# Seven of the gate layers' 32 row pairs computed in seven products, and the last down sets' combined products added to the residual earlier

## The chip, the cores and the metric

The kernel runs on one core of a Trainium2 chip. The metric is device time in microseconds (us) of one execution; the time before is 2294.47, the median of 3 runs (2294.33 to 2295.38). The profile is of one further execution.

## What is computed

The reference is a two-layer decoder trunk for 256 positions of width 2048, all in float32. What matters here is the second half of each layer:

```python
hn = rmsnorm(h, ln_mlp_g[i])
h = h + jnp.square(jax.nn.relu(hn @ mlp_w_up[i])) @ mlp_w_down[i]     # 2048 -> 8192 -> 2048
gate = jax.nn.sigmoid(rmsnorm(h, ln_ple_g[i]) @ ple_w_gate[i])        # 2048 -> 2048
h = h + gate * (p[i] @ ple_w_proj[i])                                 # 256 -> 2048
```

The first half of layer 0 is a recurrent and pooling mixer, that of layer 1 an attention mixer; a final rmsnorm closes the kernel.

## The kernel before

**Sets, pairs and steps.** A product with a 2048-row weight matrix is cut into *sets*: `mm_set` computes all 256 positions for 1024 output columns over eight *row pairs* (p = 0 to 7) of 256 weight rows. A layer's up product has eight sets, the down product eight (quarter q of the hidden width, column half n2), the gate two (`ple`, n2 = 0 and 1). A pair's weights arrive in one 1 MB load (tile `raw`, three buffers, SyncE's queue). Each pair is computed in *steps*; step s works on one weight *half* of two 512-column slices.

**The split.** A float32 product is made of three fp32r products, so every half is split: ScalarE copies it rounded into `hi` (`emit_hi`, L204), VectorE subtracts that from it into `lo` (`emit_lo`, L211). TensorE takes three products per output tile: x_hi·hi, x_lo·hi, x_hi·lo (L710, L711, L712). `hi` and `lo` have four buffers each, so the hi of step s can be written only when the products of step s-4 have read theirs.

**Plain and seven-product pairs.** A *plain* pair has two steps of 12 products, 24 in all. A pair listed in `own` is done in a Strassen-like way with seven combined products instead of eight: 21 products in four steps (3, 6, 6, 6). The third and fourth step use sums of weight blocks that VectorE makes first (`first`, L735; `second`, L740 and L741), and sums of x blocks (`ph["S"]`). Its halves are 1, 2, 2, 2 slices wide, so seven slices are split, not four. The four combined products of the last own pair are put together in `out1` to `out3` (L757 to L770) into two tiles w.

**The order of the work.** The kernel is scheduled by hand: `run` goes through the steps, and each engine does its instructions strictly in the order in which they are written:

```python
splits("sum", s + SUMS)      # weight sums, four steps ahead
splits("hi", ahead)          # hi of step s + 2
splits("lo", s)
fn(halves[s]["hi"], halves[s]["lo"])      # the products of step s
... later.pop(now) ...       # what after(n, f) has put off to this step
splits("lo", ahead)          # lo of step s + 2
```

`order` gives the pairs of a set: `TWO` is 0, 1, 4, 5, 2, 6, 3, 7 with own pairs 2 and 3, `THREE` is 0, 4, 1, 5, 2, 6, 3, 7 with own pairs 1, 2 and 3. The gate sets are plain, in order 0 to 7, with the small projection (`proj`, two steps) ahead of the fifth pair and the row scale (`rstd_of`) ahead of the sixth.

**Ends of sets.** `h_out` adds a down set's results to the residual h: `wide` (L831) adds w one and two steps after the set, `adds` (L838) the plain banks three and four steps after. Where the next product needs it (q = 3), `x_after` then transposes h (L808 on TensorE), scales it into the next x (`high` L411, `low` L874) and sums squares. For sets with own pairs in the next product, `keep` and `sums` make the S operands; before, only the sets of `out_sets` did that here. A gate set ends in `tanh` and `add` (L1056 to L1061; in layer 1 `last`, L1026 to L1034).

Of the kernel before, what the change touches and what calls it, by code (L numbers as in the profile page):

```python
# [112 lines left out]
def trunk(ctx: ExitStack, tc: tile.TileContext, a: dict, out: bass.AP):  # L113
# [573 lines left out]
    def wtiles():  # L687
        return utile().rearrange("p a b -> p (a b)").rearrange("p (n c) -> p n c", c=512), ph["w2"]

    def mm_set(src, order, X, post, own=(), S=None, between={}, hooks={}, by_n=None):  # L690


        B, n_set = ph["B"], ph["sets"]
        ph["sets"] += 1
        order = list(order)
        roles = {r: (i + 4 * n_set) % 8 for i, r in enumerate(PLAIN[0] + PLAIN[1] + OWNR)}
        begun = set()
        owned = [p for p in order if p in own]
        last = {r: owned[-1] if r in OWNR else order[-1] for r in roles if owned or r not in OWNR}
        w = {}  # L700

        def acc_of(r):
            while len(B) <= roles[r]:
                B.append(bank())
            return B[roles[r]]

        def product(r, x, hi, lo, n, end):
            b = acc_of(r)
            x_hi, x_lo = x
            pe.matmul(b, lhsT=x_hi, rhs=hi[:, n, :], start=r not in begun, stop=False, skip_group_check=True)  # L710
            pe.matmul(b, lhsT=x_lo, rhs=hi[:, n, :], start=False, stop=False, skip_group_check=True)  # L711
            pe.matmul(b, lhsT=x_hi, rhs=lo[:, n, :], start=False, stop=end, skip_group_check=True)  # L712
            begun.add(r)

        def A(p, k, t):
            x = X(2 * p + k)
            return x[:, t * P:(t + 1) * P], x[:, T + t * P:T + (t + 1) * P]

        def plain(p, k):
            def fn(hi, lo):  # L720
                for n in range(2):
                    for t in range(2):
                        product(PLAIN[t][n], A(p, k, t), hi, lo, n, k == 1 and p == order[-1])
                if k == 1 and p == order[-1]:
                    post(w.get("w"), [[acc_of(PLAIN[t][n]) for n in range(2)] for t in range(2)])
            return fn

        def own_fns(p):
            def sx(x):
                v = ph["S"][S][p][:, x - 1, :]  # L730
                return v[:, :P], v[:, P:]

            def first(raw):
                t = w["t"] = slot()
                dve.tensor_tensor(t, raw[:, 0::3, :], raw[:, 1:2, :].to_broadcast([P, 2, 512]), op=OP.add)  # L735
                return t

            def second(raw):
                t = slot()
                dve.tensor_tensor(t[:, 0], w["t"][:, 0], raw[:, 3], op=OP.add)  # L740
                dve.tensor_tensor(t[:, 1], t[:, 0], raw[:, 2], op=OP.add)  # L741
                return t

            def fn(*what):
                def f(hi, lo):
                    for n, (r, x) in enumerate(what):
                        product(r, x() if callable(x) else sx(x), hi, lo, n, False if r in PLAIN[0] + PLAIN[1] else p == last[r])
                    if p == owned[-1] and what[0][0] == "P6":
                        for d, g in enumerate((out1, out2, out3)):
                            after(d, g)  # L750
                return f
            return [(0, 1, None, fn(("Q1", lambda: A(p, 0, 0)))),
                    (2, 2, None, fn(("Q2", lambda: A(p, 1, 0)), ("P3", 4))),
                    (0, 2, first, fn(("Q5", 1), ("P7", 3))),
                    (0, 2, second, fn(("P6", 2), ("P4", lambda: A(p, 1, 1))))]

        def out1():  # L757
            w1, w2 = w["w"] = wtiles()
            for to, r in ((w1[:, 0], "Q1"), (w2[:, 0], "P7"), (w2[:, 1], "Q5")):
                act.activation(to, acc_of(r), AF.Copy)  # L760
            dve.tensor_tensor(w1[:, 1], acc_of("P6"), w1[:, 0], op=OP.subtract)

        def out2():
            w1, w2 = w["w"]
            dve.scalar_tensor_tensor(w2[:, 0], w2[:, 0], -1.0, w1[:, 1], op0=OP.mult, op1=OP.subtract)
            dve.tensor_tensor(w1[:, 1], w1[:, 1], w2[:, 1], op=OP.subtract)

        def out3():
            w1, w2 = w["w"]
            dve.scalar_tensor_tensor(w2[:, 1], w2[:, 0], -1.0, w2[:, 1], op0=OP.mult, op1=OP.subtract)  # L770

        def column(p, n):

            def fn(hi, lo):
                for k in range(2):
                    for t in range(2):
                        product(PLAIN[t][n], A(p, k, t), hi, lo, k, k == 1 and p == order[-1])
                if p == order[-1]:
                    splits("lo", state["step"] + 2)
                    by_n(n, [acc_of(PLAIN[t][n]) for t in range(2)])  # L780
            return fn

        for i, p in enumerate(order):
            if by_n and i == len(order) - 2:
                us = [len(loads), len(loads) + 1]
                for q in order[i:]:
                    loads.append({"src": src(q), "nk": 4, "w": 512})
                for n in range(2):
                    for u, q in zip(us, order[i:]):
                        halves.append({"at": (u, slice(n, 4, 2), 2)})  # L790
                        steps.append(("w", len(halves) - 1, column(q, n)))
                return
            if i in between:
                between[i]()
            if i in hooks:
                add_hook(hooks[i])
            parts = own_fns(p) if p in own else [(0, 2, None, plain(p, 0)), (2, 2, None, plain(p, 1))]
            add_blocks(src(p), parts)
# [19 lines left out]

    TWO, THREE = ((2, 3), (0, 1, 4, 5, 2, 6, 3, 7)), ((1, 2, 3), (0, 4, 1, 5, 2, 6, 3, 7))

    def h_out(n2, r, X, gi, sx=None, w_first=True):

        def post(w, banks):
            hb = lambda t, n: h[:, t, n2 * 1024 + n * 512:n2 * 1024 + (n + 1) * 512]

            def wide(t):
                ht = h[:, t, n2 * 1024:(n2 + 1) * 1024].rearrange("p (n c) -> p n c", c=512)
                if r is None:
                    dve.tensor_tensor(ht, ht, w[t], op=OP.add)
                else:  # L830
                    dve.scalar_tensor_tensor(ht, w[t], r[:, t:t + 1], ht, op0=OP.mult, op1=OP.add)  # L831

            def adds(n):
                for t in range(2):
# [4 lines left out]
            if w is not None and X is None:  # L839
# [2 lines left out]
                after(4, lambda: wide(0))  # L842
                after(8, lambda: wide(1))
                return
            at = 0 if w is None else 3
            for t in range(0 if w is None else 2):
                after(1 + t, lambda t=t: wide(t))
            for n in range(2):
                after(at + n, lambda n=n: adds(n))
# [71 lines left out]
    def mlp(l, X, Xn):  # L921
# [66 lines left out]
        for q in range(4):  # L988
            for n2 in range(2):
                post = up_out(q, n2)  # L990
                if q == 0 and n2 == 0:
                    post = (lambda post: lambda w, banks: (after(0, r2_of), post(w, banks)))(post)
                own, order = THREE if q and n2 == 0 else TWO
                mm_set(lambda p, q=q, n2=n2: a["mlp_w_up"][l][q][n2][p], order, X, post, own, 0)
            for n2 in range(2):
                own, order = THREE if n2 and q < 3 else TWO
                mm_set(lambda p, q=q, n2=n2: a["mlp_w_down"][l][n2][8 * q + p], order, H,
                       h_out(n2, R2, Xn if q == 3 else None, G_PLE + 16 * l), own, 1)

    def ple(l, X, Xn):  # L1000
        st = {}
# [12 lines left out]
        def gate(n2):  # L1014
# [2 lines left out]
            gb = lambda n: st["g"][:, n2 * 1024 + n * 512:n2 * 1024 + (n + 1) * 512]  # L1017
            hg = lambda t, n: st["hg"][:, t, n2 * 1024 + n * 512:n2 * 1024 + (n + 1) * 512]

            def last(n, banks):  # L1020

                W = st.setdefault("W", None) or wtiles()
                st["W"] = W if n == 0 else None
                end = n2 == 1 and n == 1
                for t in range(2):
                    act.activation(W[t][:, n], banks[t], AF.Tanh, scale=HALF[:, t:t + 1])  # L1026

                def add(t):
                    dve.scalar_tensor_tensor(W[t][:, n], W[t][:, n], 1.0, eb(t, n), op0=OP.add, op1=OP.mult)
# [1 line left out]
                    last_square(t, n2, n)  # L1031

                def times_gain(t):
                    dve.tensor_tensor(hg(t, n), hb(t, n), gb(n), op=OP.mult)  # L1034
                if end:
                    add(0)
# [9 lines left out]

            def post(w, banks):
                if l == 1:
                    for n in range(2):
                        after(2 * n, lambda n=n: last(n, [banks[t][n] for t in range(2)]))  # L1050
                    return
                W = wtiles()

                def tanh(n):
                    for t in range(2):
                        act.activation(W[t][:, n], banks[t][n], AF.Tanh, scale=HALF[:, t:t + 1])  # L1056

                def add(n):
                    for t in range(2):
# [10 lines left out]
        def load_e():  # L1070
            st["e"] = big(F32, (P, 2, D))
            if l == 1:
                st["g"] = big(F32, (P, 2, D))[:, 0]
                st["hg"] = big(F32, (P, 2, D))
                g = a["gfin"]
                nc.scalar.dma_start(st["g"], g.to_broadcast([P, D]))

# [22 lines left out]
        add_hook(load_e)  # L1100
        for n2 in range(2):
            post, last = gate(n2)
            mm_set(lambda p, n2=n2: a["ple_w_gate"][l][n2][p], range(8), X, post, between={4: lambda n2=n2: proj(n2)},
                   hooks={5: rstd_of} if n2 == 0 else {}, by_n=last if l == 1 and n2 == 1 else None)
        add_hook(ph["close"])

# [341 lines left out]
```

## Time and profile before

| | |
|---|---|
| median of 3 runs | 2294.47 us |
| the profiled execution | 2295.85 us |
| its span, first to last instruction | 2293.8 us |
| TensorE (PE) busy | 2269.0 us, 99% |
| VectorE (DVE) busy | 1797.9 us, 78% |
| ScalarE (ACT) busy | 1340.6 us, 58% |
| DMA, mean | 190 GB/s |
| granted TensorE clock, mean | 0.998 |

PE is TensorE's matmul, PEld its weight load, DVE VectorE, ACT ScalarE, SP SyncE. L204 is line 204 of the kernel. A row of a timeline gives the start (us from the span's start), the length, engine, line, operation, tiles written and read, shape and count; in brackets the idle time ahead of it and what ended it. Matmuls are pipelined: their lengths overlap, and the distance of two starts is what one takes.

### The profile page before, as it was taken

How to read it: one execution, taken by the hardware profiler on the slowest of the kernel's cores; microseconds unless marked ns; L12 is line 12 of the kernel's file. 1: busy time of each engine (PE TensorE's matmuls, PEld its weight loads, DVE VectorE, ACT ScalarE, POOL GpSimd, SP SyncE). 2: the span in 40 equal slices, each digit the busy share in tenths (PEclk: the TensorE clock that was granted, in tenths of full speed). 3: DMA queues.
4: the chain of work that ended last, by engine and by line, in shares of the span. 5: the costliest groups of instructions: out<-in, count | busy, mean ns of one | idle time of the engine just before them, and what ended most of it. 6: DMA issues, size and time to landing. Idle time of an engine off the chain costs nothing.

```text
span 2293.8 us, 30360 instructions
## 1 busy us (share of the span) xinstructions
PE 2269.0 (99%) x11506; PEld 1927.0 (84%) x11506; DVE 1797.9 (78%) x2475; ACT 1340.6 (58%) x1940; POOL 14.6 (1%) x42
## 2 busy tenths in 40 slices
PE   8999999999999999999999999999999999999997
PEld 8998888888888888889889988888888888888886
DVE  6786688988988987856875676688988988988865
ACT  6665565565566565665564454566566565565654
POOL 2000000000000000000000000000000000000000
PEclk9999999999999999999999999999999999999999
DMA  7645555555555555555775224555555555555553
GB/s 259 213 155 179 204 184 202 202 184 200 204 184 196 206 185 199 187 183 204 255 275 177 87 93 159 176 184 200 190 198 196 192 199 194 194 199 191 204 194 129
DMA packets 69539, 436.58 MB, mean 190 GB/s; under 512 B 9872, under 2 KB 14352, under 8 KB 18448
## 3 DMA queue, kind: packets, MB, share of 16 engines
q1 hardware_dynamic: 64832, 427.90, 54.0%
q10 hardware_dynamic: 4560, 6.74, 0.9%
q8 instruction: 90, 1.47, 0.3%
q14 instruction: 57, 0.47, 0.1%
HBM read 432.51 MB, written 2.10 MB: 189 GB/s over the span
## 4 chain that ended last, share of the span: by engine, by line
PE 97%; DVE 1%; DMA 0%; ACT 0%; issue 0%; SPq 0%; DVEq 0%; ACTq 0%
PE ps L712 25%; PE ps L710 25%; PE ps L711 25%; PE ps L295 11%; PE ps L299 3%; PE ps L808 2%; PE ps L1390 1%; PE ps L300 1%; PE ps L1180 1%; PE ps L963 0%; DVE lo L211 0%; DMA raw<-in_ab_w_in 0%; PE ps L1332 0%; PE ps L1330 0%; PE ps L1333 0%; PE ps L588 0%
## 5 line engine op out<-in xcount | busy, mean ns | idle before, releaser
L211 DVE TENSOR_TENSOR lo<-raw,hi 128x1024 fp32r<-128x1024 f32 (+1 forms) x817 | 935.9, 1158 | 159.1 <-ACT hi L204 158.4
L204 ACT ACTIVATE hi<-raw 128x1024 fp32r<-128x1024 f32 (+1 forms) x817 | 813.3, 1008 | 382.8 <-PE ps L711 300.5
L710 PE MATMUL ps<-hi,big 128*128 128x512 f32 x2436 | 954.5, 392 | 0.0
L712 PE MATMUL ps<-lo,big 128*128 128x512 f32 x2436 | 948.8, 389 | 0.0
L711 PE MATMUL ps<-hi,big 128*128 128x512 f32 x2436 | 948.1, 389 | 0.0
L712 PEld LDWEIGHTS ps<-lo,big 128*128 128x128 f32 x2436 | 457.2, 188 | 96.2 <-DVE lo L211 0.6
L711 PEld LDWEIGHTS ps<-hi,big 128*128 128x128 f32 x2436 | 457.5, 188 | 92.9
L710 PEld LDWEIGHTS ps<-hi,big 128*128 128x128 f32 x2436 | 457.4, 188 | 92.8
L204 ACT ACTIVATE hi<-big 128x1024 fp32r<-128x1024 f32 x152 | 161.4, 1062 | 253.3 <-PE ps L711 213.2
L295 PE MATMUL ps<-big,hi 128*128 128x256 f32 x1408 | 264.5, 289 | 7.7 <-ACT hi L204 7.7
L211 DVE TENSOR_TENSOR lo<-big,hi 128x1024 fp32r<-128x1024 f32 x152 | 185.8, 1222 | 90.8 <-ACT hi L204 90.8
L295 PEld LDWEIGHTS ps<-big,hi 128*128 128x128 f32 x1408 | 223.1, 193 | 9.7 <-ACT hi L204 7.7
L295 PE MATMUL ps<-big,lo 128*128 128x256 f32 x704 | 200.5, 285 | 1.0 <-DVE lo L211 0.9
L295 PEld LDWEIGHTS ps<-big,lo 128*128 128x128 f32 x704 | 135.8, 193 | 1.6 <-DVE lo L211 1.6
L299 PE MATMUL ps<-big,hi 128*128 128x512 f32 x320 | 113.6, 398 | 0.0
L735 DVE TENSOR_TENSOR big<-raw 128x1024 f32<-128x1024 f32 x76 | 92.6, 1219 | 0.4 <-DMA raw<-in_mlp_w_down 0.2
L300 PE MATMUL ps<-big,lo 128*128 128x256 f32 x320 | 89.7, 280 | 0.6 <-DVE lo L211 0.5
L299 PEld LDWEIGHTS ps<-big,hi 128*128 128x128 f32 x320 | 60.1, 188 | 14.1
L950 DVE TENSOR_TENSOR big<-ps,big 128x512 fp32r<-128x512 f32 x64 | 41.1, 684 | 36.6 <-ACT big L946 36.6
L300 PEld LDWEIGHTS ps<-big,lo 128*128 128x128 f32 x320 | 60.3, 189 | 2.0 <-DVE lo L211 1.5
L411 ACT ACTIVATE big<-ps,gains 128x256 fp32r<-128x256 f32 x80 | 31.2, 472 | 42.6 <-PE ps L808 42.6
L741 DVE TENSOR_TENSOR big<-big,raw 128x512 f32<-128x512 f32 x76 | 52.6, 692 | 2.6
(256 smaller groups left out, 1630.2 us busy)
## 6 DMA issues: line engine op xcount, KB each, us to landing
raw<-in_mlp_w_up SPq DMA_DIRECT2D x128, 1024.0 KB, 4.9
raw<-in_mlp_w_down SPq DMA_DIRECT2D x128, 1024.0 KB, 4.9
raw<-in_c_w_in SPq DMA_DIRECT2D x36, 1024.0 KB, 4.9
raw<-in_ple_w_gate SPq DMA_DIRECT2D x32, 1024.0 KB, 4.9
raw<-in_ab_w_in SPq DMA_DIRECT2D x20, 1024.0 KB, 4.9
raw<-in_ab_w_out SPq DMA_DIRECT2D x16, 1024.0 KB, 4.9
raw<-in_c_w_out SPq DMA_DIRECT2D x16, 1024.0 KB, 4.9
raw<-in_c_cmp_w_k SPq DMA_DIRECT2D x8, 1024.0 KB, 4.9
```

The costliest lines, as they stand in the source:

```text
L204: act.activation(halves[s]["hi"][:, k, :w], halves[s]["src"][:, k, :], AF.Copy)
L211: dve.tensor_tensor(lo[:, k, :w], src[:, k, :], halves[s]["hi"][:, k, :w].bitcast(F32), op=OP.subtract)
L295: pe.matmul(b, lhsT=wt[:, kk, cols], rhs=x[:, x0:x0 + T], start=first and n == 0 and j % 2 == 0, stop=last and n == 2, skip_group_check=True)
L299: pe.matmul(b, lhsT=hi[:, kk, cols], rhs=x, start=first, stop=False, skip_group_check=True)
L300: pe.matmul(b[:, T:], lhsT=lo[:, kk, cols], rhs=x[:, :T], start=False, stop=last, skip_group_check=True)
L710: pe.matmul(b, lhsT=x_hi, rhs=hi[:, n, :], start=r not in begun, stop=False, skip_group_check=True)
L711: pe.matmul(b, lhsT=x_lo, rhs=hi[:, n, :], start=False, stop=False, skip_group_check=True)
L712: pe.matmul(b, lhsT=x_hi, rhs=lo[:, n, :], start=False, stop=end, skip_group_check=True)
L735: dve.tensor_tensor(t, raw[:, 0::3, :], raw[:, 1:2, :].to_broadcast([P, 2, 512]), op=OP.add)
L741: dve.tensor_tensor(t[:, 1], t[:, 0], raw[:, 2], op=OP.add)
L808: pe.transpose(b[:, j, t * P:(t + 1) * P], of(t, i // 2, (2 * i + j) % 4), ident)
L950: dve.tensor_tensor(Hs[n2][:, k:k + 2, T:], scratch(banks, i), Hs[n2][:, k:k + 2, :T].bitcast(F32), op=OP.subtract)
```

## The change

- Gate sets use own pairs: 2 and 3 in the first set of either layer (order 0, 1, 4, 5, 6, 2, 3, 7), 1, 2 and 3 in the second set of layer 0 (0, 4, 5, 1, 6, 2, 3, 7, with the projection now ahead of the third pair). The second set of layer 1, the kernel's last, stays plain. That is seven of 32 pairs.
- The four down sets of q = 3 take the order 0, 1, 4, 5, 2, 3, 6, 7, add w to h during pairs 6 and 7 (`early`), and do `adds` and all of `x_after` three steps earlier. The first of each two also makes the S operands for the gate.
- The gate sets' ends add w to the banks (two more additions per 512 columns) ahead of the tanh; in layer 1 the tile `hg` is taken later.

```diff
@@ mm_set, own_fns
                     if p == owned[-1] and what[0][0] == "P6":
                         for d, g in enumerate((out1, out2, out3)):
                             after(d, g)
+                        for t in range(2 if early else 0):
+                            after(3 + t, lambda t=t: early(t, w["w"]))
@@ h_out
-            at = 0 if w is None else 3
-            for t in range(0 if w is None else 2):
+            at = 3 if w is not None and w_first else 0
+            for t in range(2 if at else 0):
                 after(1 + t, lambda t=t: wide(t))
@@ mlp
                 own, order = THREE if n2 and q < 3 else TWO
+                if q == 3:
+                    order = (0, 1, 4, 5, 2, 3, 6, 7)
                 mm_set(lambda p, q=q, n2=n2: a["mlp_w_down"][l][n2][8 * q + p], order, H,
-                       h_out(n2, R2, Xn if q == 3 else None, G_PLE + 16 * l), own, 1)
+                       h_out(n2, R2, Xn if q == 3 else None, G_PLE + 16 * l, 0 if q == 3 else None, q < 3), own, 1,
+                       early=(lambda t, w, n2=n2: h_wide(n2, R2, t, w)) if q == 3 else None)
@@ ple, gate: post (layer 0; layer 1 alike in last)
                 def tanh(n):
                     for t in range(2):
-                        act.activation(W[t][:, n], banks[t][n], AF.Tanh, scale=HALF[:, t:t + 1])
+                        if w:
+                            dve.tensor_tensor(W[t][:, n], banks[t][n], W[t][:, n], op=OP.add)
+                    for t in range(2):
+                        act.activation(W[t][:, n], W[t][:, n] if w else banks[t][n], AF.Tanh, scale=HALF[:, t:t + 1])
@@ ple
-            mm_set(lambda p, n2=n2: a["ple_w_gate"][l][n2][p], range(8), X, post, between={4: lambda n2=n2: proj(n2)},
+            own, order, at = (((2, 3), (0, 1, 4, 5, 6, 2, 3, 7), 4), ((1, 2, 3), (0, 4, 5, 1, 6, 2, 3, 7), 2))[n2]
+            if l == 1 and n2 == 1:
+                own, order, at = (), range(8), 4
+            mm_set(lambda p, n2=n2: a["ple_w_gate"][l][n2][p], order, X, post, own, 0, between={at: lambda n2=n2: proj(n2)},
                    hooks={5: rstd_of} if n2 == 0 else {}, by_n=last if l == 1 and n2 == 1 else None)
```

VectorE's instructions in layer 0's first down set of q = 3, from the splits of pair 2's second half to those of pair 3's last (L211 is a lo; L735, L740 and L741 are the weight sums). Before:

```order
L211 TENSOR_TENSOR lo<-big,hi 128x1024 x2
L211 TENSOR_TENSOR lo<-raw,hi 128x1024 x2
L735 TENSOR_TENSOR big<-raw 128x1024
L211 TENSOR_TENSOR lo<-raw,hi 128x512
L740 TENSOR_TENSOR big<-big,raw 128x512
L741 TENSOR_TENSOR big<-big,raw 128x512
L211 TENSOR_TENSOR lo<-raw,hi 128x1024
L211 TENSOR_TENSOR lo<-big,hi 128x1024 x2
```

Changed:

```order
L211 TENSOR_TENSOR lo<-big,hi 128x1024 x2
L735 TENSOR_TENSOR big<-raw 128x1024
L211 TENSOR_TENSOR lo<-raw,hi 128x512
L740 TENSOR_TENSOR big<-big,raw 128x512
L741 TENSOR_TENSOR big<-big,raw 128x512
L211 TENSOR_TENSOR lo<-raw,hi 128x1024
L211 TENSOR_TENSOR lo<-big,hi 128x1024 x2
```

The two lo of pair 6 no longer stand between the own pairs: pair 3's sums follow at once on pair 2's last lo.

VectorE in the second down set of q = 3, up to the splits of its pair 2 (in the changed listing the first L211 is the split of the eighth step). Before:

```order
L874 SCALAR_TENSOR_TENSOR big<-ps,gains,big 128x256 x4
L211 TENSOR_TENSOR lo<-raw,hi 128x1024
L735 TENSOR_TENSOR big<-raw 128x1024
L211 TENSOR_TENSOR lo<-raw,hi 128x512
L740 TENSOR_TENSOR big<-big,raw 128x512
L741 TENSOR_TENSOR big<-big,raw 128x512
L211 TENSOR_TENSOR lo<-raw,hi 128x1024
```

Changed:

```order
L817 TENSOR_TENSOR big<-big 128x2x128 x4
L211 TENSOR_TENSOR lo<-raw,hi 128x1024
L735 TENSOR_TENSOR big<-raw 128x1024
L891 TENSOR_TENSOR big<-big 128x8x128
L211 TENSOR_TENSOR lo<-raw,hi 128x512
L740 TENSOR_TENSOR big<-big,raw 128x512
L741 TENSOR_TENSOR big<-big,raw 128x512
L211 TENSOR_TENSOR lo<-raw,hi 128x1024
L211 TENSOR_TENSOR lo<-big,hi 128x1024 x2
L735 TENSOR_TENSOR big<-raw 128x1024
```

L817 and L891 (`sums`) are new here, and L891 stands between the eighth step's split and pair 2's.

VectorE from the end of layer 0's first gate set into the second. Before:

```order
L1060 SCALAR_TENSOR_TENSOR u<-u,big 128x512
L1061 TENSOR_TENSOR h<-h,u 128x512
L1060 SCALAR_TENSOR_TENSOR big<-big 128x512
L1061 TENSOR_TENSOR h<-h,big 128x512
L211 TENSOR_TENSOR lo<-raw,hi 128x1024
```

Changed:

```order
L211 TENSOR_TENSOR lo<-raw,hi 128x1024
L772 SCALAR_TENSOR_TENSOR big<-big 128x512
L1068 TENSOR_TENSOR u<-ps,u 128x512
L1068 TENSOR_TENSOR big<-ps,big 128x512
L1074 SCALAR_TENSOR_TENSOR u<-u,big 128x512
L1075 TENSOR_TENSOR h<-h,u 128x512
L1074 SCALAR_TENSOR_TENSOR big<-big 128x512
L1075 TENSOR_TENSOR h<-h,big 128x512
L211 TENSOR_TENSOR lo<-raw,hi 128x1024
```

L772 is `out3`, the end of combining the own pairs; L1068 adds w to the banks, and the tanh (on ScalarE, between L1068 and L1074) now waits for it.

## Rows read from the trace of the kernel before

**Rows 1.** The page's parts 1 and 4: busy time by engine; the chain that ended last.
```profile
PE 2269.0 (99%) x11506; PEld 1927.0 (84%) x11506; DVE 1797.9 (78%) x2475; ACT 1340.6 (58%) x1940; POOL 14.6 (1%) x42
...
PE 97%; DVE 1%; DMA 0%; ACT 0%; issue 0%; SPq 0%; DVEq 0%; ACTq 0%
```
**Rows 2.** Waits of PE (us in total, times, longest), the longest of five rows.
```profile
PE ps L295 <- ACT hi L204: 7.7, 1, 7.7
```
**Rows 3.** Timeline of PE: first and last of 148 rows; later, a pair 2's first product.
```profile
879.57 0.39 PE L710 MATMUL ps<-hi,big 128*128 128x512 f32 x1
...
912.89 0.39 PE L710 MATMUL ps<-hi,big 128*128 128x512 f32 x1
...
2114.65 0.39 PE L710 MATMUL ps<-hi,big 128*128 128x512 f32 x1
```
**Rows 4.** Timeline of DVE around pair 2 of layer 1's first q = 3 down set.
```profile
2106.03 1.22 DVE L735 TENSOR_TENSOR big<-raw 128x1024 f32<-128x1024 f32 x1
2107.18 0.69 DVE L211 TENSOR_TENSOR lo<-raw,hi 128x512 fp32r<-128x512 f32 x1
2107.79 0.68 DVE L740 TENSOR_TENSOR big<-big,raw 128x512 f32<-128x512 f32 x1
2108.51 0.69 DVE L741 TENSOR_TENSOR big<-big,raw 128x512 f32<-128x512 f32 x1
...
2115.77 1.23 DVE L211 TENSOR_TENSOR lo<-big,hi 128x1024 fp32r<-128x1024 f32 x1 [1.50 <-ACT hi L204]
2116.91 2.35 DVE L211 TENSOR_TENSOR lo<-raw,hi 128x1024 fp32r<-128x1024 f32 x2
```
**Rows 5.** Timeline of ACT, the hi of that pair's fourth step.
```profile
2114.68 1.06 ACT L204 ACTIVATE hi<-big 128x1024 fp32r<-128x1024 f32 x1 [1.66 <-PE ps L711]
```
**Rows 6.** Timeline of all engines: a step of layer 1's second output set.
```profile
1450.80 1.23 DVE L211 TENSOR_TENSOR lo<-raw,hi 128x1024 fp32r<-128x1024 f32 x1
...
1451.60 0.39 PE L710 MATMUL ps<-hi,big 128*128 128x512 f32 x1
...
1452.42 0.40 PE L710 MATMUL ps<-hi,big 128*128 128x512 f32 x1
```
**Rows 7.** The same set: PE's first transposes; DVE's eighth split and the row behind.
```profile
1441.66 1.03 PE L808 MATMUL ps<-ident,h 128*128 128x128 f32 x8
...
1457.47 1.22 DVE L211 TENSOR_TENSOR lo<-raw,hi 128x1024 fp32r<-128x1024 f32 x1
1458.68 1.23 DVE L889 TENSOR_TENSOR big<-big 128x1024 fp32r<-128x1024 f32 x1
```
**Rows 8.** Layer 0's first gate set: PE, then ACT and DVE around the row scale.
```profile
962.49 1.03 PE L808 MATMUL ps<-ident,h 128*128 128x128 f32 x8
963.28 0.48 PE L710 MATMUL ps<-hi,big 128*128 128x512 f32 x1
963.60 0.40 PE L711 MATMUL ps<-hi,big 128*128 128x512 f32 x1
...
978.08 2.02 ACT L204 ACTIVATE hi<-raw 128x1024 fp32r<-128x1024 f32 x2
...
981.46 0.15 DVE L377 TENSOR_REDUCE rs<-ssq 128x2 f32<-128x8 f32 x1
...
981.85 1.99 ACT L204 ACTIVATE hi<-raw 128x1024 fp32r<-128x1024 f32 x2
```
**Rows 9.** Ends of a set: an up set's addition; layer 0's first gate set on ACT, DVE, PE.
```profile
859.13 0.68 DVE L932 TENSOR_TENSOR u<-ps,u 128x512 f32<-128x512 f32 x1
...
997.07 0.69 ACT L1056 ACTIVATE u<-ps,rs 128x512 f32<-128x512 f32 x1 [1.27 <-PE ps L712]
...
997.79 0.69 DVE L1060 SCALAR_TENSOR_TENSOR u<-u,big 128x512 f32<-128x512 f32 x1 [4.75 <-ACT u L1056]
998.52 0.69 DVE L1061 TENSOR_TENSOR h<-h,u 128x512 f32<-128x512 f32 x1
...
1001.63 1.03 PE L808 MATMUL ps<-ident,h 128*128 128x128 f32 x8
```

More of the change, by code (lines that the diff above doesn't have):

```diff
@@ L688, in wtiles, with mm_set @@
         return utile().rearrange("p a b -> p (a b)").rearrange("p (n c) -> p n c", c=512), ph["w2"]
-    def mm_set(src, order, X, post, own=(), S=None, between={}, hooks={}, by_n=None):
+    def mm_set(src, order, X, post, own=(), S=None, between={}, hooks={}, by_n=None, early=None):
         B, n_set = ph["B"], ph["sets"]
@@ L819, in trunk, with h_wide @@
     TWO, THREE = ((2, 3), (0, 1, 4, 5, 2, 6, 3, 7)), ((1, 2, 3), (0, 4, 1, 5, 2, 6, 3, 7))
+    def h_wide(n2, r, t, w):
+        ht = h[:, t, n2 * 1024:(n2 + 1) * 1024].rearrange("p (n c) -> p n c", c=512)
+        dve.scalar_tensor_tensor(ht, w[t], r[:, t:t + 1], ht, op0=OP.mult, op1=OP.add)
     def h_out(n2, r, X, gi, sx=None, w_first=True):
@@ L826, in wide @@
             def wide(t):
[L827 to L831, printed above, removed]
+                h_wide(n2, r, t, w)
             def adds(n):
@@ L1018, in gate, with last @@
             hg = lambda t, n: st["hg"][:, t, n2 * 1024 + n * 512:n2 * 1024 + (n + 1) * 512]
-            def last(n, banks):
+            def last(n, banks, add_w=False):
                 W = st.setdefault("W", None) or wtiles()
@@ L1025, in last @@
                 for t in range(2):
-                    act.activation(W[t][:, n], banks[t], AF.Tanh, scale=HALF[:, t:t + 1])
+                    if add_w:
+                        dve.tensor_tensor(W[t][:, n], banks[t], W[t][:, n], op=OP.add)
+                for t in range(2):
+                    act.activation(W[t][:, n], W[t][:, n] if add_w else banks[t], AF.Tanh, scale=HALF[:, t:t + 1])
                 def add(t):
@@ L1033, in times_gain @@
                 def times_gain(t):
+                    if "hg" not in st:
+                        st["hg"] = big(F32, (P, 2, D))
                     dve.tensor_tensor(hg(t, n), hb(t, n), gb(n), op=OP.mult)
@@ L1048, in post @@
                 if l == 1:
+                    st["W"] = w
                     for n in range(2):
-                        after(2 * n, lambda n=n: last(n, [banks[t][n] for t in range(2)]))
+                        after(2 * n, lambda n=n: last(n, [banks[t][n] for t in range(2)], w is not None))
                     return
-                W = wtiles()
+                W = w or wtiles()
                 def tanh(n):
                     for t in range(2):
-                        act.activation(W[t][:, n], banks[t][n], AF.Tanh, scale=HALF[:, t:t + 1])
+                        if w:
+                            dve.tensor_tensor(W[t][:, n], banks[t][n], W[t][:, n], op=OP.add)
+                    for t in range(2):
+                        act.activation(W[t][:, n], W[t][:, n] if w else banks[t][n], AF.Tanh, scale=HALF[:, t:t + 1])
                 def add(n):
@@ L1073, in load_e @@
                 st["g"] = big(F32, (P, 2, D))[:, 0]
-                st["hg"] = big(F32, (P, 2, D))
                 g = a["gfin"]
```

## The prediction

> **What bounds the kernel now.** I read the busy shares and the chain that ended last first: PE is busy for 99% of the span and is 97% of the chain [rows 1]. Then I read what PE waited for. That list has five rows, and the longest wait, 7.7 us, lies at the kernel's start [rows 2]; in the down sets of q = 3 and the gate sets PE waits for nothing. Its products there follow one another evenly: 148 rows from 879.57 to 912.89, so 33.32 / 147 = 0.2267 us each [rows 3]. A plain step is 12 x 0.2267 = 2.72 us, a plain pair 5.44, an own pair 21 x 0.2267 = 4.76. So a product less is worth 0.2267 us, and any operand that comes late costs its lateness in full.
>
> **What is removed.** Seven pairs lose three products each: 21 x 0.2267 = **4.76 us** saved. The product count is certain, since pairs in the list of own pairs issue 3 + 6 + 6 + 6. The Trainium skill (TensorE: Matmul & The Clock Gate, Back-to-back issue gap) gives about 131 ns for a sustained 512-column product in a stream of weight loads and matmuls, which would make the saving 21 x 0.131 = 2.75 us. The row says 0.2267, and the row decides.
>
> Adding w to h earlier saves nothing by itself, as PE waited for none of it. It is needed because the gate now reaches pair 4, whose x come from the second down set, in step 5 instead of step 11. The loads are the same, each 1 MB on SP's queue, with three raw buffers; only which pair they bring changes, and a load is asked for two pairs ahead, so I cost them at nothing. POOL has no part. The tile hg is taken later, after its predecessor's readers; nothing. The new ACT work (keep) stands in ACT's queue at the same steps as in the output sets, and its cost is in the second item below.
>
> **What is added on DVE.** An own pair puts on DVE the sums (L735, L740, L741) and seven slices of lo instead of four. Held times, start to next start, are: L735 1.15 us, a 512-wide lo 0.61, L740 0.72 (the next one needs its result), L741 0.61 like the 512-wide lo, a 1024-wide lo 1.14, its length 1.23 [rows 4]. How much lateness is free? In one place before, a lo ended at 1452.03, which is 0.43 after its step's first product, and the next product came at 1452.42 rather than at 1451.60 + 3 x 0.2267 = 1452.28 [rows 6]. So a lo may end 0.43 - 0.14 = 0.29 us after the step's start, and beyond that costs its lateness.
>
> *Two own pairs in a row, first down set.* Pair 2's first product is at 2114.65 [rows 3]. Its last hi starts at 2114.68, released by PE, because it must wait for a free hi buffer [rows 5], and its last lo starts at 2115.77 [rows 4], 1.12 after the pair. So DVE cannot be further ahead at that point. By the order listing pair 3's L735, lo, L740, L741 and lo now follow at once: the second lo of pair 3 ends 1.12 + 1.14 + 1.15 + 0.61 + 0.72 + 0.61 + 1.23 = 6.58 after pair 2's start. PE starts that step after one own pair and three products, 4.76 + 0.68 = 5.44, plus 0.29 free: 5.73. Late by **0.85 us**. The following steps are on time (lo every 1.14, steps of 1.36). Before, pair 6 stood between: 5.44 us of PE for 2.28 of DVE. This occurs in each layer's first q = 3 down set and in layer 0's second gate set: 3 x 0.85 = 2.55.
>
> The Trainium skill (VectorE: DVE Perf Modes, The DRAIN you can't avoid) says that the next operation does not start until the pipeline is empty. If that meant the reported end, the chain would be 1.23 + 1.22 + 0.69 + 0.68 + 0.69 + 1.23 = 5.74 instead of 5.46, and each of these places 0.28 later. The rows show the next lo starting at 2116.91, 0.09 before the one from 2115.77 ends.
>
> *Second down set, with the sums for the gate.* The same work at the same steps stands in layer 1's second output set: first transposes at 1441.66, so the set starts one step earlier at 1438.94, and DVE is in its eighth lo at 1457.47, 18.53 in, with everything before it already late against ACT [rows 7]. From there the listing gives: that lo 1.14, L735 1.15, L891 1.14 (its twin L889 is 1.23 long, like a lo [rows 7]), lo 0.61, L740 0.72, L741 0.61, three lo 3.42, L735 1.15, lo 0.61, L740 0.72, L741 0.61, lo 1.23, which ends at 31.64. PE starts that step after eight plain steps (21.76), two groups of transposes of 0.88 (0.79, and a first product 0.09 longer [rows 8]), an own pair of 4.76 and 0.68 for three products, at 28.96, plus 0.29. Late by **2.4 us** in each layer: 4.8. DVE does not idle in between, so nothing gives this back.
>
> *First gate set.* The projection ends 28.96 into the set (ten steps and 1.76). ACT copies it out: in the rows the set's fifth step starts at 962.49 with transposes, so the projection ends at 962.49 + 0.88 + 5 x 2.72 = 976.97, and the next hi starts at 978.08, 1.11 later [rows 8]. In the changed kernel this hi and the next (0.5, half of 1.01, and 1.01) are those of pair 2; DVE's lo, L740, L741, lo take from 30.6 to 33.7, and only behind them stands the row scale's reduction. ACT's next hi comes 0.39 after that reduction (981.46 to 981.85): 34.1, the one after 35.1 to 36.15; DVE's last lo of pair 2 to 37.3, then L735, lo, L740, L741 and a lo to 41.6. PE is there at 28.96 + 5.44 + 4.76 + 0.68 = 39.84, plus 0.29. Late by **1.5 us**, in both layers: 3.0.
>
> *Ends of gate sets.* Counted from x, the end of that late lo: PE ends its step at x + 1.07 (1.36 less 0.29), the pair at x + 3.79, the set at x + 9.23, and the first transposes are due at x + 11.95. DVE does three lo, then waits for the combined products to x + 3.4, L763 0.61, lo 1.14, L767 and L768 1.33, lo 1.14, L772 0.61, to x + 8.2; then two L1068 (0.68 long, as L932), behind the first of them a tanh of 0.69, and two pairs of 0.73 and 0.61 for h [rows 9]: h is ready at x + 12.4. Late by 0.45. The second half is another lo, two L1068, tanh and four operations, ready at x + 17.6, while PE asks at x + 16.0: 1.6 more. Before, h was ready well ahead of 1001.63, with the first tanh already at 997.07 [rows 9]. Together **2.1 us** after layer 0's first gate set, and the same after its second, where layer 1's projection follows: 4.2. In layer 1 nothing is transposed there, but the fourth step's lo stands behind the second tanh group: due at x + 17.7, ends at x + 18.6, so 0.9.
>
> **The sum.** 2.55 + 4.8 + 3.0 + 4.2 + 0.9 = 15.45 us of new waits, less 4.76: **10.7 us slower**. Against the profiled execution's own 2295.85 us that is 2306.55; it is 1.38 above the median of the runs, so for the median I forecast 2294.47 + 10.7 = **2305.2 us**. Bounds of what no row shows: the waits at the ends of sets lie between 0 (if tanh and additions slip into gaps that I don't see) and 5.1, and I take the upper end because each engine's queue is in strict order there; the two-in-a-row waits lie between 0 and 0.85 + 0.28.
>
> **Rivals.** A measurement of this kernel can tell about 0.2%, 4.6 us, from no change.
>
> *Faster: DVE keeps up.* If pair 3's sums and lo were done in time at all seven places, only the saving would be left: 2294.47 - 4.76 = 2289.7. For it: DVE is busy for 78% only [rows 1]. Against it: it idles because it waits for hi, and hi for a buffer [rows 4, 5]. The point that decides is 0.85 us per place; the total of waits must stay below 0.2 us for the gain to be over 0.2%. 5 in 100.
>
> *No change: only the two-in-a-row waits.* Seven times 0.85 is 5.95, less 4.76: 2295.7. This needs the gate's sums, the row scale and the tanh to be hidden behind the same wait. 11 in 100.
>
> *Slower, but the ends of sets are hidden.* Without their 5.1: 2300.1. 14 in 100.
>
> *Slower still: DVE's operations do not overlap by 0.09.* 0.28 at seven places and more in the long chains, some 2.5 us: 2307.7; the rule of the skill above would act so, and the rows speak against it. 4 in 100. Waits of DVE that I have not found (a slot, a bank of the projection) would go the same way, to 2309.5: 4 in 100.
>
> That the change does not do what it says is excluded by the listing: both the products and the order are there.
>
> **The numbers.** The forecast itself has 62 in 100. The range reaches from 2298.5, under the case with hidden ends, to 2309.5; what lies outside is the faster case and the one without change, 16 in 100. Faster 0.05, same 0.11, slower 0.84.
>
> **What would show it.** PE's list of waits should gain rows of L712 released by DVE's lo L211, of 0.9 to 2.4 us, some nine of them, all in own pairs that follow an own pair; and L808 released by DVE's L1075. PE's products should be 21 fewer at the same 0.2267 us. If those L712 rows are absent or below 0.3 us, my reading of the order is wrong. If they are there but the total stays near 6 us, the second and third item are wrong; if the L808 rows are absent, the handover is.

## Result and the profile after

The changed kernel takes 2306.73 us, the median of 4 runs (2306.09 to 2307.17), beside 2294.70 for the kernel before: a ratio of 1.0051, 95% interval 1.0039 to 1.0064. It is **slower** by 0.5%, and the interval lies above 1. The profiled execution took 2306.49 us (span 2304.4, granted clock 0.998), 10.6 above that of before.

The page after, parts 1 and 4, against [rows 1]:

```profile
PE 2269.2 (98%) x11485; PEld 1922.1 (83%) x11485; DVE 1849.0 (80%) x2554; ACT 1362.7 (59%) x1979; POOL 14.6 (1%) x42
...
PE 94%; DVE 3%; issue 1%; ACT 1%; DMA 0%; SPq 0%; DVEq 0%; ACTq 0%
```

PE has 21 matmuls less and is busy as long as before: recorded lengths overlap, so part of each wait counts as busy (below, 1.09 us are lost where 0.82 is idle). DVE is busy 51 us longer and is now 3% of the chain. Waits of PE after, against [rows 2] (us in total, times, longest):

```profile
PE ps L712 <- DVE lo L211: 7.9, 8, 1.4
PE ps L295 <- ACT hi L204: 7.5, 1, 7.5
PE ps L810 <- DVE h L1075: 2.7, 5, 1.0
```

The row at the kernel's start is nearly as before; the other two are new. Layer 0's first q = 3 down set shows how such a wait comes about. DVE, then PE, at pair 3, against [rows 4]:

```profile
884.29 1.23 DVE L211 TENSOR_TENSOR lo<-big,hi 128x1024 fp32r<-128x1024 f32 x1 [1.77 <-ACT hi L204]
885.43 1.22 DVE L735 TENSOR_TENSOR big<-raw 128x1024 f32<-128x1024 f32 x1
886.57 0.68 DVE L211 TENSOR_TENSOR lo<-raw,hi 128x512 fp32r<-128x512 f32 x1
887.17 0.68 DVE L740 TENSOR_TENSOR big<-big,raw 128x512 f32<-128x512 f32 x1
887.88 0.69 DVE L741 TENSOR_TENSOR big<-big,raw 128x512 f32<-128x512 f32 x1
888.50 1.22 DVE L211 TENSOR_TENSOR lo<-raw,hi 128x1024 fp32r<-128x1024 f32 x1
```
```profile
888.56 0.39 PE L711 MATMUL ps<-hi,big 128*128 128x512 f32 x1
889.77 0.50 PE L712 MATMUL ps<-lo,big 128*128 128x512 f32 x1 [0.82 <-DVE lo L211]
890.10 0.40 PE L710 MATMUL ps<-hi,big 128*128 128x512 f32 x1
```

DVE waited 1.77 us for a hi at 884.29, and from there on works without a pause; the lo that PE needs at 888.79 (888.56 + 0.2267) ends at 889.72. PE loses 0.98, and another 0.11 in front of the next product: 1.09 us. All waits below are told so, as the extra distance between PE's starts, with what is lost in front of the next product where nothing else is said.

The handover behind layer 0's first gate set, DVE after, against [rows 9]:

```profile
1004.37 0.69 DVE L1075 TENSOR_TENSOR h<-h,big 128x512 f32<-128x512 f32 x1
1004.98 1.22 DVE L211 TENSOR_TENSOR lo<-raw,hi 128x1024 fp32r<-128x1024 f32 x1
1006.12 0.68 DVE L1068 TENSOR_TENSOR u<-ps,u 128x512 f32<-128x512 f32 x1
...
1009.64 0.69 DVE L1075 TENSOR_TENSOR h<-h,big 128x512 f32<-128x512 f32 x1
1010.25 1.22 DVE L211 TENSOR_TENSOR lo<-raw,hi 128x1024 fp32r<-128x1024 f32 x1
```

From one lo to the next DVE takes 5.27 us, for the lo itself and six operations with 0.2 us of pause, while a step with its transposes is 2.72 + 0.88 = 3.60 of PE. The transposes wait for h:

```profile
1010.39 0.98 PE L810 MATMUL ps<-ident,h 128*128 128x128 f32 x7 [1.00 <-DVE h L1075]
```

### The profile page after: what moved, and what is told of

Read it like the earlier page. It is cut to its first block, busy times and chain, and to the rows that moved or that the text cites. A ratio compares the mean times of both kernels' runs of the same rounds, so it can differ in the third digit from the quotient of the medians.

```text
span 2304.4 us, 30461 instructions
## 1 busy us (share of the span) xinstructions
PE 2269.2 (98%) x11485; PEld 1922.1 (83%) x11485; DVE 1849.0 (80%) x2554; ACT 1362.7 (59%) x1979; POOL 14.6 (1%) x42
## 4 chain that ended last, share of the span: by engine, by line
PE 94%; DVE 3%; issue 1%; ACT 1%; DMA 0%; SPq 0%; DVEq 0%; ACTq 0%
PE ps L712 24%; PE ps L710 24%; PE ps L711 24%; PE ps L295 10%; PE ps L299 3%; PE ps L810 2%; DVE lo L211 2%; PE ps L1406 1%; PE ps L300 1%; PE ps L1196 1%; PE ps L965 0%; DMA raw<-in_ab_w_in 0%; PE ps L1348 0%; PE ps L1346 0%; PE ps L1349 0%
## 5 line engine op out<-in xcount | busy, mean ns | idle before, releaser
L211 DVE TENSOR_TENSOR lo<-raw,hi 128x1024 fp32r<-128x1024 f32 (+1 forms) x817 | 932.0, 1152 | 140.5 <-ACT hi L204 139.8
L712 PE MATMUL ps<-lo,big 128*128 128x512 f32 x2425 | 946.1, 390 | 8.1 <-DVE lo L211 7.9
L712 PEld LDWEIGHTS ps<-lo,big 128*128 128x128 f32 x2425 | 455.2, 188 | 108.7 <-DVE lo L211 13.7
L204 ACT ACTIVATE hi<-big 128x1024 fp32r<-128x1024 f32 x166 | 176.0, 1061 | 258.4 <-PE ps L711 201.7
L211 DVE TENSOR_TENSOR lo<-big,hi 128x1024 fp32r<-128x1024 f32 x166 | 201.8, 1222 | 88.3 <-ACT hi L204 88.3
L735 DVE TENSOR_TENSOR big<-raw 128x1024 f32<-128x1024 f32 x83 | 101.0, 1217 | 0.4 <-DMA raw<-in_mlp_w_down 0.4
L741 DVE TENSOR_TENSOR big<-big,raw 128x512 f32<-128x512 f32 x83 | 57.5, 692 | 2.9
L740 DVE TENSOR_TENSOR big<-big,raw 128x512 f32<-128x512 f32 x83 | 56.6, 682 | 0.0
```

The source lines that it names most:

```text
L204: act.activation(halves[s]["hi"][:, k, :w], halves[s]["src"][:, k, :], AF.Copy)
L211: dve.tensor_tensor(lo[:, k, :w], src[:, k, :], halves[s]["hi"][:, k, :w].bitcast(F32), op=OP.subtract)
```

## Experiments

Two theories. **A, the order:** DVE's work would fit behind PE's, but stands in its strict queue in lumps (two own pairs in a row; S sums ahead of an own pair; six operations between two lo at a gate's end), and PE pays each lump's lateness. **B, the amount:** an own pair in these sets brings more DVE work than PE's products cover, wherever it stands. Every kernel was timed beside the kernel before (medians 2294.96 to 2295.05 us).

**e1: the gate sets plain again; the down sets as changed.**

```diff
-            own, order, at = (((2, 3), (0, 1, 4, 5, 6, 2, 3, 7), 4), ((1, 2, 3), (0, 4, 5, 1, 6, 2, 3, 7), 2))[n2]
+            own, order, at = (), range(8), 4
```

The first q = 3 down sets also make no S operands. 

> Edit: the gate sets are plain again (order 0 to 7, no S operands made for them); the down sets of q = 3 keep the new order with pairs 2 and 3 in a row and the early addition. Theory A (a seven-product pair right behind another makes its lo late, because DVE's queue is in strict order): nothing is saved, and each of the four down sets waits once, about 0.85 to 1.1 us, as the sums for the gate are gone from the second ones: some 3.8 us slower than before, about 2298.5, with no wait in the gate sets and none of L810. Rival B (the loss lies in the gates' seven-product pairs and their work, not in the order): as before, 2294.6, with no waits.

Measured: 2298.83 us, ratio 1.0016 (1.0008 to 1.0025). PE's waits for lo:

```profile
PE ps L712 <- DVE lo L211: 2.5, 4, 0.8
```

They are four, one in each q = 3 down set, of 1.11, 0.81, 0.81 and 0.81. So the new order of the down sets costs by itself, without an own pair in the gates, and the S sums made the second down sets' waits larger.

**e2: a plain pair between the own pairs of the first q = 3 down sets.**

```diff
-                    order = (0, 1, 4, 5, 2, 3, 6, 7)
+                    order = (0, 1, 4, 5, 2, 3, 6, 7) if n2 else (0, 1, 4, 2, 5, 3, 6, 7)
```

> Edit: in the first down set of q = 3 of each layer the order is 0, 1, 4, 2, 5, 3, 6, 7: the same pairs in the same ways, with plain pair 5 between the two seven-product pairs. Theory A: the wait of L712 in these two sets (1.1 and 0.8 us in the changed kernel) is gone, everything else stays: 1.9 us faster than the changed kernel, about 2304.8. Rival B: no change against the changed kernel, 2306.7.

Measured: 2304.20 us, ratio 1.0040 (1.0027 to 1.0053), span 2.0 below the changed kernel's. The waits of these two sets are gone, all others stand. The same work in another order costs nothing: A, at this place.

**e3: the row scale ahead of the eighth pair, not the sixth.**

```diff
-                   hooks={5: rstd_of} if n2 == 0 else {}, by_n=last if l == 1 and n2 == 1 else None)
+                   hooks={7: rstd_of} if n2 == 0 else {}, by_n=last if l == 1 and n2 == 1 else None)
```

> Edit: the row scale (reduction, square root, reciprocal) of the first gate set is computed ahead of its last pair instead of ahead of pair 2. Theory A: the wait behind the two own pairs of that set falls from 1.54 us to the 0.85 of two own pairs in a row, in both layers: 1.4 us faster than the changed kernel, about 2305.3. If the wait were only that of the pairs, it stays 1.5 and the time 2306.7.

Measured: 2306.39 us, ratio 1.0049 (1.0036 to 1.0063): no gain. The wait at the gate's pair 3 did fall, from 1.54 to 0.82, but the handover's grew:

```profile
PE ps L810 <- DVE h L1075: 3.4, 5, 1.0
```

against 2.7 in the change, and a new wait for lo of 0.77 came at 2242.59. What is moved within a queue that has no pause is late at the next place.

**e4: the transposes at layer 0's gate ends one step later.**

```diff
-                x_after(n2, banks, Xn, G_MIX + 16)
+                x_after(n2, banks, Xn, G_MIX + 16, at=1)
```

> Edit: at the end of layer 0's two gate sets the transposes of h and all that follows them come one step later. Theory A: PE asks for h 2.7 us later than now, so the waits of L810 on DVE's L1075 (2.2 us after the first set, 1.7 after the second) are gone: 3.9 us faster than the changed kernel, about 2302.8; if the projection's banks, which these transposes use, come free too late, up to 1 us comes back as a wait at the projection. Rival B: no change, 2306.7.

Measured: 2309.15 us, ratio 1.0061 (1.0049 to 1.0074): a miss, 2.4 us the other way. DVE there:

```profile
1004.80 1.22 DVE L211 TENSOR_TENSOR lo<-raw,hi 128x1024 fp32r<-128x1024 f32 x1
1005.94 0.68 DVE L1068 TENSOR_TENSOR u<-ps,u 128x512 f32<-128x512 f32 x1
...
1010.08 2.35 DVE L211 TENSOR_TENSOR lo<-raw,hi 128x1024 fp32r<-128x1024 f32 x2
```

DVE does the same at nearly the same times. Without the transposes in front, PE came earlier to the products that read these lo, and waited for them: 1.38 us up to 1006.08, 1.64 up to 1011.35, and three more waits (1.43, 1.54, 0.95) at the entry of layer 1, whose 128x256 products come 0.12 us apart where nothing is late. That is 6.9 us for the 4.3 of the handovers that went. Not the transposes were misplaced; the lo stood behind the group.

**e5: own pairs 2 and 3 apart in the gate sets, the projection ahead of the third pair.**

```diff
-            own, order, at = (((2, 3), (0, 1, 4, 5, 6, 2, 3, 7), 4), ((1, 2, 3), (0, 4, 5, 1, 6, 2, 3, 7), 2))[n2]
+            own, order, at = (((2, 3), (0, 1, 4, 2, 5, 3, 6, 7), 2), ((2, 3), (0, 4, 1, 2, 5, 3, 6, 7), 2))[n2]
```

> The gate sets alone are reordered: own pairs 2 and 3 in all three, in order 0, 1, 4, 2, 5, 3, 6, 7 (layer 0's second set 0, 4, 1, 2, 5, 3, 6, 7), a plain pair between them and two behind them, the projection ahead of the third pair; six own pairs, not seven, so 0.68 us of products come back. Theory A (waits arise because own pairs stand next to each other and end one pair before the set does): the first gate sets' waits (1.54 us each) and the second's (0.81) go, and the two handovers (2.2 and 1.7) shrink to about a third since the combined products are put together two pairs earlier: about 2300.2 us. Rival B (a gate set with own pairs simply holds more VectorE work than it can hide, wherever the pairs stand): the waits only move to other steps, about 2306 to 2307.

Measured: 2300.25 us, ratio 1.0022 (1.0013 to 1.0031). The waits inside the gate sets and at layer 1's gate end are gone, and of each handover only its second half is left. The order is not the only thing that differs: pair 1 of layer 0's second gate set is plain here.

**e6: the second q = 3 down sets with one own pair.**

```diff
-                    order = (0, 1, 4, 5, 2, 3, 6, 7)
+                    own, order = ((2,), (0, 1, 4, 5, 6, 2, 3, 7)) if n2 else (own, (0, 1, 4, 5, 2, 3, 6, 7))
```

> The second down sets of q = 3 compute pair 2 alone in seven products, in order 0, 1, 4, 5, 6, 2, 3, 7; pair 3 is plain (three products more in each, 2 x 0.68 = 1.36 us). Theory A (the wait of 2.2 us is VectorE's backlog from the S sums and the transposed x, shown at pair 3's sums because they follow pair 2's at once): the waits go, 2 x 2.2 less 1.36, about 2303.7 us. Rival B (the backlog alone delays pair 2 too, and the wait only moves there): between 2306 and 2308.

Measured: 2303.34 us, ratio 1.0036 (1.0024 to 1.0049). No wait is left at pair 2 or 3 of these sets. Pair 2 is still an own pair behind the same S sums, one plain pair later, and its 0.41 us are gone; so the backlog is worked off by then. Pair 3's wait went together with its own work, so for it this run does not tell order and amount apart.

**e7: one weight sum twice.**

```diff
                 t = slot()
+                if early and p == owned[-1]:
+                    dve.tensor_tensor(t[:, 0], w["t"][:, 0], raw[:, 3], op=OP.add)
```

> In the four down sets of q = 3 one 512-column weight sum of pair 3 (L740) is done twice; nothing else changes. It holds VectorE 0.61 us and stands ahead of the late lo. Theory A (the late lo ends a chain in which VectorE does not idle): each of the four waits grows by 0.61 us, 2.4 us in all: about 2309.1 us. Rival B (the lo waits for ScalarE's hi or for a free buffer, and VectorE has room): no change, about 2306.7 us.

Measured: 2310.97 us, ratio 1.0066 (1.0054 to 1.0079). DVE in layer 0's first q = 3 down set (L741 to L743 are here what L740, L740 again and L741 are):

```profile
887.26 0.68 DVE L741 TENSOR_TENSOR big<-big,raw 128x512 f32<-128x512 f32 x1
887.97 0.69 DVE L742 TENSOR_TENSOR big<-big,raw 128x512 f32<-128x512 f32 x1
888.70 0.69 DVE L743 TENSOR_TENSOR big<-big,raw 128x512 f32<-128x512 f32 x1
889.31 1.22 DVE L211 TENSOR_TENSOR lo<-raw,hi 128x1024 fp32r<-128x1024 f32 x1
```

The sum held DVE 0.71 to 0.73 us, not 0.61, and the four waits grew by that: 0.98 to 1.71, 1.56 to 2.28, 0.70 to 1.43, 1.54 to 2.27 (each without the 0.11 behind it), 2.9 us in all. The profiled execution is 2.9 above the change's (2309.37 to 2306.49). Three of the five runs lie some 2 us higher still; they were not profiled.

**e8: e2, e5 and e6 together.** 

> e2's first down sets, e6's second down sets and e5's gate sets together: six own pairs in the gates, two fewer in the down sets, so 4 x 0.68 = 2.72 us of products less than in the kernel before. Theory A (the costs add up place by place): waits of about 1.5 us are left at the ends of gate sets: about 2293.7 us, the first version that is no slower than the kernel before. Rival B (VectorE's work returns as waits elsewhere): above 2298 us.

Measured: 2295.11 us, ratio 0.9999 (0.9990 to 1.0008). The waits add up place by place, as A has it. Of PE's waits one row is left that the kernel before does not have:

```profile
PE ps L810 <- DVE h L1075: 1.8, 2, 1.0
```

They cost 1.33 and 1.23 us, more than the 1.5 expected, so 2.72 - 2.56 = 0.2 us of gain is left, too little to be seen.

**e9: e8 with e4's edit.** 

> e8 with e4's edit: the transposes at layer 0's gate ends one step later. In e4 VectorE worked without a pause from the last own pair into the next set, so waits for h became waits for lo. Theory A (e4 failed for VectorE's backlog alone): with the own pairs apart VectorE idles 2.2 us just ahead of the set's end (e8's timeline at 996.00), so the two handover waits (1.1 and 0.9 us) go and nothing takes their place: about 2293.2 us. Rival B (the end's own chain of additions and tanh delays the next lo wherever the own pairs stand): waits for lo of 1 to 1.5 us at each handover, 2295 us or above.

Measured: 2297.72 us, ratio 1.0012 (1.0003 to 1.0021): theory A as stated there fell. DVE in e9 behind layer 0's first gate set:

```profile
995.70 0.69 DVE L1068 TENSOR_TENSOR u<-ps,u 128x512 f32<-128x512 f32 x1 [2.23 <-PE ps L712]
...
999.85 1.22 DVE L211 TENSOR_TENSOR lo<-raw,hi 128x1024 fp32r<-128x1024 f32 x1
...
1005.12 2.35 DVE L211 TENSOR_TENSOR lo<-raw,hi 128x1024 fp32r<-128x1024 f32 x2
```

DVE was idle for 2.23 us, so there was no backlog from the own pairs, and still PE waited 0.51 and 1.64 here, 0.58, 1.52 and 0.95 at the entry of layer 1. The group of six alone makes the lo late.

**e12: e9 with the additions to h one step later.**

```diff
                     after(n, lambda n=n: tanh(n))
-                    after(n, lambda n=n: add(n))
+                    after(1 + n, lambda n=n: add(n))
```

> e9 with the additions to h put off by one step at layer 0's two gate ends, so that VectorE does a lo between the two L1068 and the four operations that follow the tanh; the same instructions, in another order. Theory A (the waits for lo at the gate ends, in e4 and e9, are a lo that stands behind a group of six operations; the work itself fits): the waits of 0.5, 1.6, 0.4 and 1.3 us go, the 0.74 us behind the row scale stays: 3.1 to 3.8 us below e9, about 2294.2 us. Rival B (the end holds more VectorE work than three steps of products can hide): the waits stay, about 2297.7 us.

Measured: 2293.45 us (2292.91 to 2294.09), ratio 0.9993 (0.9984 to 1.0002). DVE at the same place:

```profile
996.37 0.69 DVE L1068 TENSOR_TENSOR big<-ps,big 128x512 f32<-128x512 f32 x1
996.98 1.22 DVE L211 TENSOR_TENSOR lo<-raw,hi 128x1024 fp32r<-128x1024 f32 x1
998.11 0.69 DVE L1074 SCALAR_TENSOR_TENSOR u<-u,big 128x512 f32<-128x512 f32 x1
...
1001.37 0.68 DVE L1068 TENSOR_TENSOR big<-ps,big 128x512 f32<-128x512 f32 x1
1001.97 1.21 DVE L211 TENSOR_TENSOR lo<-raw,hi 128x1024 fp32r<-128x1024 f32 x1
1003.10 0.68 DVE L1074 SCALAR_TENSOR_TENSOR u<-u,big 128x512 f32<-128x512 f32 x1
```

A lo now stands between the two additions of w and the four operations behind the tanh. PE waits nowhere at the first handover, and once at layer 1's entry, 0.98 us behind the row scale. So the waits are 4.2 us less than in e9, and the median is 4.3 less. The page's first row:

```profile
PE 2266.4 (99%) x11494; PEld 1924.0 (84%) x11494; DVE 1836.2 (80%) x2539; ACT 1358.5 (59%) x1973; POOL 14.8 (1%) x42
```

DVE does 38 us more than before [rows 1] and hides nearly all of it. So B falls for the first down sets, for gates with six own pairs and for their ends; in the second down sets only one own pair was tried without a wait, and for two, as for the seventh in the gates, it stays open. It is the only version that comes out below the kernel before: all its 11 runs lie below the lowest of the 15 beside it (2294.56), but the interval still takes in 1, so 1.6 us is the size to be told, not a proven gain.

**e10 and e11: e5's gates, the down sets as before, w added later (e11 with e4's edit too).**

```diff
-            at = 3 if w is not None and w_first else 0
+            at = 0 if w is None else 3 if w_first else 2
+            for n in range(2):
+                after(at + n if w_first else n, lambda n=n: adds(n))
@@ mlp
-                if q == 3:
-                    order = (0, 1, 4, 5, 2, 3, 6, 7)
```

The diff shows the two main places; `early` and the old place of `adds` go too. In both runs the projection overwrites banks from which the low parts of the gate's last x are still to be made (in e10 its products start at 964.15, and L876 makes those parts from 966.59). So they do not compute the reference's result; the amount of work is that of the full computation, and only the times are read here. 

> The gate sets of e5 (own pairs apart, six in all), but the down sets of q = 3 in the order of before (0, 1, 4, 5, 2, 6, 3, 7), both own pairs, without the early addition: w is added one and two steps after the set as before, the plain banks at the set's end, the transposes begin two steps later than in the change. Six own pairs are won and none lost: 6 x 0.68 = 4.08 us of products less than before. Theory A (only adjacent own pairs and S sums right ahead of one cost anything): the second down sets wait about 0.4 us each at pair 2, the handovers 2.0 together, and the gate's pair 4, now with x that come two steps later, up to 0.5 in each layer: about 2293.8 us. Rival B (without the early addition the gate waits for pair 4's x or for its own pair 2): 2 us or more in each layer, above 2296 us.

 

> e10 with e4's edit too. Theory A: e10 less the two handover waits, about 1.9 us below e10. Rival B as in e9: no gain over e10.

Measured: 2302.12 us, ratio 1.0029 (1.0017 to 1.0041), and 2304.04, ratio 1.0039 (1.0026 to 1.0051). The gate does not wait for pair 4's x, so B's reason falls, but its time comes nearer: the S sums of pairs 2 and 3, now two steps later, stand inside the second down sets' pair 2 (L817 at 927.86, between L741 and the late lo), and PE waits 2.33 us for its lo (2.32 in layer 1, both without what follows), not 0.4. e11 gains nothing over e10, as e9 does not over e8. What followed the wait is told in the last section.

## Why the prediction was right

The forecast was 2305.2 us; measured are 2306.73, inside the range, and slower as forecast. Term by term, from the extra distances between PE's starts:

| term | predicted, us | measured, us |
|---|---|---|
| products | -4.76 | -4.76: 21 fewer, at 0.2267 away from waits |
| own pairs in a row, 3 places | 2.55 | 1.09 + 0.81 + 0.81 = 2.71 |
| second down sets | 4.8 | 2.19 + 2.17 = 4.36 |
| first gate sets | 3.0 | 1.54 + 1.54 = 3.08 |
| handovers of layer 0's gates | 4.2 | 2.20 + 2.09 = 4.29 |
| layer 1's gate end | 0.9 | 0.95 |
| net | +10.7 | +10.6 |

The spans differ by 10.6 too, but this agreement is partly luck. The first of each two rows is a product ahead of everything that the change touches, the second the kernel's last one. Before, then changed:

```profile
209.96 0.39 PE L710 MATMUL ps<-hi,big 128*128 128x512 f32 x1
2278.81 0.39 PE L712 MATMUL ps<-lo,big 128*128 128x512 f32 x1
```
```profile
209.19 0.39 PE L710 MATMUL ps<-hi,big 128*128 128x512 f32 x1
2289.43 0.39 PE L712 MATMUL ps<-lo,big 128*128 128x512 f32 x1
```

The changed kernel's profiled execution came 0.77 us earlier through the part that both kernels share, and before's is the latest of the 14 profiled ones there; from there to the end it lost 2080.24 - 2068.85 = 11.4 us. The terms explain 10.6 of them. Part of the missing 0.8 are the some ten products behind each wait, which come 0.02 to 0.06 us late in all; the rest stays open.

- **Two own pairs in a row.** Place, engine and size are right; e2 removes the wait by order alone, and e7 moves it by what is put into the chain. The list of waits shows eight rows of L712, at the places that the forecast priced (some nine were named); the one at layer 1's gate end is not in an own pair, against the wording of the sign.
- **Second down sets.** I had one wait of 2.4 at pair 3. The trace has 0.41 at pair 2 already, 1.67 at pair 3 and 0.11 at a plain step. A first wait delays PE, so the second is smaller; the total was 0.4 oversized.
- **First gate sets.** The row scale does stand in the chain (e3 took 0.72 of 1.54 away), but moving it gave nothing back.
- **Handovers.** The size is right and the cause was incomplete. I priced h as late for the transposes. e4, e9 and e12 show that the lo behind the same six operations is late too, and waits as soon as the transposes give way.
- **The median.** The forecast was 1.5 us low, and by its numbers that is the offset: I took 1.38 off because before's profiled execution lay that far above its median, but the change's lay 0.24 below its own. Some 0.7 of the 1.38 would be before's late start of the rows above, an accident of one execution.
- **The rivals.** "DVE keeps up", "only the two-in-a-row waits" and "the ends of sets are hidden" fall: the waits that they leave out are in the trace. The chance that DVE's operations do not overlap falls with the rows above: L735 at 885.43 is 1.22 long, and the next operation starts 1.14 later, in layer 0 too.

## What to carry to other kernels

When the bound engine is busy for 99%, a step that takes work from it and gives it to an engine that is busy for 80% is priced by where the new work stands in that engine's queue, not by its busy share: write the queue between two operands that the bound engine needs, and compare its length with the steps in between. Spread such lumps so that an operand's producer stands between them; the same instructions cost 5.2 us of waits in one order and 1.0 in another (e9, e12). Moving the consumer of a late result, instead of the lump in front of it, only let the next operand be late here (e4, e9).

## What the runs showed of the hardware

**The clock fell after a long stall.** PE in e10, second q = 3 down set of layer 0:

```profile
928.05 0.39 PE L711 MATMUL ps<-hi,big 128*128 128x512 f32 x1
930.60 0.65 PE L712 MATMUL ps<-lo,big 128*128 128x512 f32 x1 [2.17 <-DVE lo L211]
931.05 0.63 PE L710 MATMUL ps<-hi,big 128*128 128x512 f32 x1
931.47 0.63 PE L711 MATMUL ps<-hi,big 128*128 128x512 f32 x1
...
934.35 0.39 PE L712 MATMUL ps<-lo,big 128*128 128x512 f32 x1
```

and the stretches behind it (us, busy PE, PEld, DVE, ACT, POOL, then the granted clock, DMA share, GB/s):

```profile
931.00:934.00 3.00, 3.00 (x8) 2.22 (x7) 3.00 (x4) 3.00 (x4) 0.00 (x0) 0.50 0.77 254
934.00:940.00 6.00, 6.00 (x27) 4.97 (x26) 5.96 (x8) 3.05 (x4) 0.00 (x0) 0.98 0.57 193
```

Behind a wait of 2.33 us the granted clock was 0.50, that is 1.2 GHz, and products came 0.43 us apart; nine distances took 3.75 us where 9 x 0.2267 = 2.04 would have done. The Trainium skill (TensorE: Matmul & The Clock Gate, Wait — 56ns, not 53.3ns?) gives 426.7 ns for 512 columns at that level, which these rows bear out. The clock fell likewise behind e10's wait of 2.32 us in layer 1 and e11's second one (2.33, granted clock 0.50 from 2168 to 2171). Waits of 2.28 us (e7) and the first of e11's (2.32) were not followed by it. So a wait of this length can cost 1.7 us more than itself, and not always. That three of e7's runs were some 2 us slower would fit, but was not shown.

**A wait costs a little more than itself.** The product behind nearly every late lo starts 0.11 us later than 0.2267 after the one that waited (890.10 - 889.77 = 0.33 us), and the some ten behind it lose another 0.02 to 0.06 in all (0.06 behind 992.57 in the changed kernel).
